# Post-norm rounds regrouped, two first pieces behind the last transposes, and one sum moved behind a split, in a single-core decoder layer

## The chip, the cores and the metric

One core of a Trainium2 chip runs the whole layer. The metric is the device time of one execution in microseconds (us). The kernel before takes 1078.08 us, the median of 3 runs (1076.54 to 1078.99).

## What is computed

One layer of a decoder trunk, in float32, for 1024 positions of width 1024. Cut to what matters here:

```python
y = mixing_sublayer(h, ...)                  # pooling and dilated attention, then @ w_out
x = x + gt_m * rms_norm(y, g_post_mix)       # residual after the first sub-layer
h = rms_norm(x, g_pre_ffn) * (1.0 + sc_f) + sh_f
up = h @ w_up                                # 1024 x 1024 by 1024 x 5632
gate, val = up[..., :D_FF], up[..., D_FF:]   # D_FF = 2816
gate = causal_conv3(gate, conv_w) + conv_b
y = (gelu(gate) * val) @ w_down
x = x + gt_f * rms_norm(y, g_post_ffn)
```

`rms_norm` divides a row by the root of its mean square. Everything that the change touches lies between `@ w_out` and the first blocks of `h @ w_up`.

## The kernel before, in words

**Splits.** A float32 operand of a large product is split into a high and a low part, and three matmuls (high by high, high by low, low by high) replace one. ScalarE (ACT) writes the high part as a rounded copy (L120), VectorE (DVE) the low part as a difference (L167). A pair of such parts of a 128x512 weight is called a piece here. PE can use the high part as soon as ACT has written it, and needs the low part one matmul later.

**The out-projection and the first norm.** Positions are cut into 8 tiles of 128. `y_part` (L592 to L594) issues three matmuls of a tile's product with `w_out`; 8 of these make a tile, in two of the eight accumulator banks. Tiles 0 to 3 have the bank pairs 0-1, 2-3, 4-5 and 6-7. `stats(t)` is called after each tile and works a round: it loads the residual's rows `xr` (L881, issued by SyncE's queue, SP), squares y of tile t on ACT with a sum (L884), squares x1 of tile t-1 on ACT (L889), takes the root (L149), refines both reciprocals in five tiny DVE instructions (L163, L156 to L159), writes x1 = y times its factor times a gate row (L894, which is the last to read the tile's banks), adds the residual (L895), stores x1 (L896), and scales x1 of tile t-1 into `xr` (L898). That last result is what the up-projection needs.

**The turns.** The scaled rows must be transposed. A turn (`x_turn`, L905) is 8 PE transposes of two tiles' `xr` into banks 6 and 7, and `h_split` copies them out on ACT (L913, 4 copies) into `raw_a` or `raw_b`, which hold a quarter of the transposed h each. `TURN_AT` says before which slot each turn stands: slot (t, n) is the n-th `y_part` of tile t, and from t = 8 on the n-th group of three matmuls (L1016 to L1018) of the first products of the up-projection, block c = t - 8. The block with c = 3 writes into banks 6 and 7, so it starts after the last turn's copies. The first turn writes into the banks of y's tile 3, so it starts after that tile's L894.

**The first blocks of the up-projection.** `h @ w_up` is done with seven products in place of eight on half-size blocks, so sums of the blocks of h (`sums`, L940), and sums of weight quarters (`start_sum`, L950, for chunk 0; `total`, L1137, on GpSimd, POOL, later) are needed. A product (n, c) is product n of column chunk c: 12 matmuls (L1066 to L1068) that take a left factor (`s` for n = 5, `s2` for 6, `s4` for 3, `s3` for 7) and a weight piece. Products (5,0), (6,0), (3,0) and (7,0) come first, then (5,1) and (6,1). `evac` adds a finished product into accumulators in SBUF (L1075 to L1085). The block `b` (`parts("22")`, 128x2048) is split for a later product. A ring of piece buffers is filled in turn: the last five are `p1` and four pieces of `more`, and `more` lies in the storage of `raw_a`, so it can be written once b's split has read that.

**Order.** On PE, ACT, DVE and POOL the order is the order of the code (`manual_schedule`); each engine works its instructions strictly in turn. Two more constants place work between the slots: at `FIRST_T`, (10,2), stand the sums and pieces of products (5,0) and (6,0) (two L950, then p from `raws` and p from `t2r`), and at `LAST_X`, (8,6), the round that only scales x1 of tile 7, and a one-element Gelu (L1008) that makes ACT load its Gelu table.

Of the kernel before, what the change touches and what calls it, by code (L numbers as in the profile page):

```python
# [68 lines left out]


NCONST = _const_layout()
LAST_X = (8, 6)
FIRST_T = (10, 2)
TURN_AT = ((5, 4, 0, 0), (6, 2, 0, 1), (6, 7, 1, 0), (7, 2, 1, 1), (8, 3, 2, 0), (8, 7, 2, 1), (9, 7, 3, 0), (10, 3, 3, 1))
# [27 lines left out]
def block_kernel(ctx: ExitStack, tc: tile.TileContext, x, pos, cols, rows, consts, w_ada_a, w_ada_b, w_in_u,  # L102
                 w_in_p, w_pool, w_out, w_up, w_down, out):
    nc = tc.nc
    cp = ctx.enter_context(tc.tile_pool(name="cp", bufs=1))
# [7 lines left out]
    PS = pp.tile([P, 8, 512], F32, name="PS")  # L113
# [25 lines left out]
    one = cp.tile([P, 1], F32, name="one")  # L139
# [362 lines left out]
    gtg = cp.tile([P, D], F32, name="gtg", tag="gtg")  # L502
# [81 lines left out]
    def y_bank(t):  # L584
        return 2 * t if t < 4 else 2 * ((t - 4) % 3)
# [281 lines left out]
    if True:  # L867
        ep = mid.enter_context(tc.tile_pool(name="ep", bufs=1))
        st8 = [{} for _ in range(NT)]
# [2 lines left out]
            for n in range(lo, hi):  # L872
                y_part(t, n % 2, n // 2)

        def stats(t):
            q = ep.tile([P, 2], F32, name="q1", tag="q1", bufs=3)
            n, d = 0, st8[t] if t < NT else None
            if t < NT:
                yv = PS[:, y_bank(t):y_bank(t) + 2, :].rearrange("p a b -> p (a b)")
                d["xr"] = ep.tile([P, D], F32, name="xr", tag="xr", bufs=6)  # L880
                nc.sync.dma_start(d["xr"], xv[:, t])  # L881
                d["x1"] = ep.tile([P, D], F32, name="x1", tag="x1", bufs=2)
                junk = ep.tile([P, D], F32, name="junk", tag="junk")
                nc.scalar.activation(junk, yv, AF.Square, accum_out=q[:, 0:1])  # L884
                n = 1
            if t:
                e = st8[t - 1]
                junk = ep.tile([P, D], F32, name="junk", tag="junk")
                nc.scalar.activation(junk, e["x1"], AF.Square, accum_out=q[:, n:n + 1])  # L889
                e["rx"] = n  # L890
                n += 1
            r = rsqrt(q[:, 0:n], root(q[:, 0:n], n), n)
            if t < NT:
                nc.vector.scalar_tensor_tensor(d["x1"], yv, r[:, 0:1], gtg, op0=ALU.mult, op1=ALU.mult)  # L894
                nc.vector.tensor_add(d["x1"], d["x1"], d["xr"])  # L895
                nc.sync.dma_start(x1v[:, t], d["x1"])  # L896
            if t:
                nc.vector.tensor_scalar_mul(e["xr"], e["x1"], r[:, e["rx"]:e["rx"] + 1])  # L898

        def x_turn(m, r):  # L900
            for i in range(4):
# [40 lines left out]
        ring, at, W, TR = [], {"p": 0, "r": 0}, {}, {}  # L942
# [5 lines left out]
        def start_sum(n, o, a, b):  # L948
            TR[n, 0] = o
            nc.vector.tensor_tensor(o, a, b, ALU.add)  # L950
# [9 lines left out]

        TURNS = {(t, n): (m, r) for t, n, m, r in TURN_AT}
        up_load(0)
# [3 lines left out]
        if True:  # L966
# [5 lines left out]
            root(cat[0][0][:, S - 1:S].bitcast(F32), scale=0.0)  # L972
            for t in range(3):
                y_mm(t, 6, 8)
                stats(t)
            for t in range(3, NT):
                for n in range(8):
                    slot((t, n))
                    y_mm(t, n, n + 1)
                stats(t)  # L980
            for c in range(AHEAD + 1):
                if c + 2 <= AHEAD:
                    up_load(c + 2)
                if c == 2:
                    raws = [rp.tile([P, 2, 512], F32, name="raws", tag="raw") for _ in range(2)]
                    raws = [t[:, i] for t in raws for i in range(2)]
                    for i in range(4):
                        nc.sync.dma_start(raws[i], w_up[0, :, i])
                    b11, b21, b12, b22 = raws
                    t2r = cp.tile([P, 512], F32, name="t2r", tag="macc")  # L990
                    p0 = r2.tile([P, 4, 512], F32R, name="p0", tag="r2b")
                    ring += [(p0[:, i], p0[:, i + 1]) for i in (0, 2)]
                    TR["t4", 0] = b21
                for n in range(8):
                    slot((8 + c, n))
                    if (8 + c, n) == FIRST_T:
                        start_sum("t1", b11, b11, b12)
                        start_sum("t2", t2r, b11, b22)
                        start_piece("t1", b11)
                        start_piece("t2", t2r)  # L1000
                    if (8 + c, n) == TURN_AT[-2][:2]:
                        sums(lo_t, range(4))
                        parts("s1", lo_t)
                        parts("s2", lo_t)
                    if (8 + c, n) == LAST_X:
                        stats(NT)
                        gelu = cp.tile([P, 1], F32, name="gelu")
                        nc.scalar.activation(gelu, one, AF.Gelu_apprx_tanh)  # L1008
# [7 lines left out]
                    nc.tensor.matmul(o, wh, ah, start=n % 4 == 0, stop=False)  # L1016
                    nc.tensor.matmul(o, wh, al, start=False, stop=False)
                    nc.tensor.matmul(o, wl, ah, start=False, stop=n % 4 == 3)  # L1018
# [3 lines left out]
            p1 = fp.tile([P, 2, 512], F32R, name="p1")  # L1022
# [35 lines left out]
            def product(n, c):  # L1058
                a, w = USES[n]
                wh, wl = W.pop((w, c))  # L1060
                used[n, c] = idle.pop(0)
                o = bank(used[n, c])
                for k in range(4):
                    ks = slice(k * P, (k + 1) * P)
                    ah, al = side(a, k)
                    nc.tensor.matmul(o, wh[:, ks], ah, start=k == 0, stop=False)  # L1066
                    nc.tensor.matmul(o, wh[:, ks], al, start=False, stop=False)  # L1067
                    nc.tensor.matmul(o, wl[:, ks], ah, start=False, stop=k == 3)  # L1068
# [33 lines left out]
            more = r1.tile(half, F32R, name="more", tag="rb2")  # L1102
# [16 lines left out]
    if True:  # L1119
# [134 lines left out]
        for hf, c in ((0, GATE_AT), (1, GATE_AT + 3)):  # L1254
            i = steps.index((5, c))
# [46 lines left out]

        prep_up(5, 5)
        parts("22", all_t)
        more = r1.tile([P, 8, 512], F32R, name="more", tag="rb0")
        ring += [(more[:, 2 * i], more[:, 2 * i + 1]) for i in range(4)] + [(p1[:, 0], p1[:, 1])]
        prep_up(6, 6)
        evac(7, 0)
        for i, (n, c) in enumerate(steps):
# [20 lines left out]
            if (n, c) == (5, NC_FF - 1):  # L1330
                more = r2.tile([P, 8, 512], F32R, name="tail", tag="r2c")
# [145 lines left out]
```

## Time and profile before

| what | value |
| --- | --- |
| median of 3 runs | 1078.08 us |
| the profiled execution: its own time | 1077.65 us |
| the profiled execution: its span | 1075.9 us |
| PE busy, share of the span | 1036.6 us, 96% |
| DVE busy | 850.9 us, 79% |
| ACT busy | 479.4 us, 45% |
| POOL busy | 223.1 us, 21% |
| mean granted PE clock | 0.992 |

The span is what the trace covers, and 1.75 us of the execution's own time lie round it. Times within the trace are counted from the span's start. A row of the timeline has the start, the duration, the engine, the line, the operation with out<-in, the shape and the count, and in brackets the idle time of the engine before it with what released it. PE matmuls are pipelined: a 128x512 matmul is shown with 0.39 us, but the next starts 0.23 us later. A row with x2, x4 or x8 holds so many instructions in succession. Names of buffers are those of the program, and `PS` is the accumulator.

### The profile page before, as it was taken

To read this page: it belongs to the slowest core of one execution; us is meant where nothing else is said; L and a number is where in the kernel's file an instruction comes from. 1 tells how busy PE (TensorE), PEld (TensorE's weight loads), DVE (VectorE), ACT (ScalarE), POOL (GpSimd) and SP (SyncE) were. 2 spreads that over 40 slices of the span, in tenths; PEclk is the share of its full clock that TensorE was granted. 3 is DMA by queue.
4 is the path that set the end of the run, shared out by engine and by line. 5 is a ranking of instruction groups with operands and counts; after the bars stand their busy time and mean duration, and the time that the engine had idled before them with its cause. 6 is when DMAs were issued, how large, how long until landed. Compare 5 with 4: busy or idle time off the path is not lost.

```text
span 1075.9 us, 15437 instructions
## 1 busy us (share of the span) xinstructions
PE 1036.6 (96%) x5174; PEld 875.5 (81%) x5174; DVE 850.9 (79%) x1845; ACT 479.4 (45%) x964; POOL 223.1 (21%) x132
## 2 busy tenths in 40 slices
PE   4999999999999989899999999999999999999997
PEld 4988988899888778677888888888878878888886
DVE  7975467875558668899999888979789999756897
ACT  6764333433354459543433333433323365544542
POOL 0000000000000000063433333333235425103460
PEclk9999999999999999899999999999999999999999
DMA  9552446362221163323344424344534889566663
GB/s 356 215 176 59 121 112 192 90 189 77 60 85 48 50 235 119 116 88 128 121 163 140 164 93 160 119 143 167 170 117 138 282 283 377 170 190 218 202 205 118
DMA packets 85148, 168.34 MB, mean 156 GB/s; under 512 B 9158, under 2 KB 25926, under 8 KB 81356
## 3 DMA queue, kind: packets, MB, share of 16 engines
q1 hardware_dynamic: 85068, 167.35, 46.9%
q8 instruction: 41, 0.67, 0.3%
q14 instruction: 39, 0.32, 0.1%
HBM read 134.47 MB, written 32.84 MB: 156 GB/s over the span
## 4 chain that ended last, share of the span: by engine, by line
PE 73%; DVE 13%; DMA 5%; ACT 5%; issue 3%; SPq 0%; DVEq 0%; ACTq 0%
PE PS L1066 9%; PE PS L1068 9%; PE PS L1067 9%; PE PS L1360 6%; PE PS L1361 6%; PE PS L1359 6%; PE PS L218 5%; PE PS L220 4%; PE PS L219 4%; PE PS L707 3%; PE PS L677 2%; DMA mraw<-in_w_ada_b_dram 2%; DVE more L1133 2%; PE PS L697 1%; DVE acc L340 1%
## 5 line engine op out<-in xcount | busy, mean ns | idle before, releaser
L1137 POOL TENSOR_TENSOR raws<-rw 128x512 f32<-128x512 f32 x30 | 49.8, 1661 | 505.8 <-DVE p L167 443.1
L218 PE MATMUL PS<-wh,hh 128*128 128x384 f32 x336 | 124.6, 371 | 0.1
L220 PE MATMUL PS<-wh,hl 128*128 128x384 f32 x336 | 113.2, 337 | 0.0
L219 PE MATMUL PS<-wl,hh 128*128 128x384 f32 x336 | 112.9, 336 | 0.0
L120 ACT ACTIVATE more<-raws 128x512 fp32r<-128x512 f32 x81 | 49.6, 624 | 70.7 <-PE PS L1067 54.3
L686 ACT ACTIVATE pm<-pm,nm 128x128 f32<-128x128 f32 (+1 forms) x96 | 42.4, 443 | 68.1 <-DVE nm L684 44.7
L1133 DVE TENSOR_TENSOR more<-raws,more 128x512 fp32r<-128x512 f32 x75 | 68.3, 913 | 3.4 <-ACT more L120 3.4
L218 PEld LDWEIGHTS PS<-wh,hh 128*128 128x128 f32 x336 | 63.4, 189 | 8.3 <-issue 4.8
L219 PEld LDWEIGHTS PS<-wl,hh 128*128 128x128 f32 x336 | 63.5, 189 | 0.6 <-issue 0.5
L220 PEld LDWEIGHTS PS<-wh,hl 128*128 128x128 f32 x336 | 63.1, 188 | 0.0
L1086 ACT ACTIVATE cv<-GG,col 128x1024 f32<-128x1024 f32 x22 | 27.4, 1245 | 73.1 <-DVE GG L1085 73.1
L1068 PE MATMUL PS<-a,more 128*128 128x512 f32 x144 | 56.3, 391 | 0.9 <-DVE more L1133 0.9
L1066 PE MATMUL PS<-a,more 128*128 128x512 f32 x144 | 56.1, 390 | 0.0
L1067 PE MATMUL PS<-a,more 128*128 128x512 f32 x144 | 56.0, 389 | 0.0
L680 DVE CUSTOM_DVE_ANT_0 pm<-PS,cst 128x128 f32<-128x128 f32 (+1 forms) x96 | 30.8, 347 | 30.6 <-PE PS L677 23.8
L1172 ACT ACTIVATE cv<-cv 128x1024 f32<-128x1024 f32 x22 | 23.4, 1062 | 62.9 <-DVE cv L1170 62.9
L1360 PE MATMUL PS<-tail 128*128 128x512 f32 x128 | 50.0, 391 | 0.5 <-DVE tail L167 0.4
L1361 PE MATMUL PS<-tail 128*128 128x512 f32 x128 | 49.8, 389 | 0.0
L1359 PE MATMUL PS<-tail 128*128 128x512 f32 x128 | 49.8, 389 | 0.0
L1168 DVE SCALAR_TENSOR_TENSOR cv<-GG,col,cv 128x1023 f32<-128x1023 f32 x22 | 35.8, 1628 | 10.8 <-ACT cv L1086 10.7
L1137 POOL TENSOR_TENSOR t2r<-raws,rw 128x512 f32<-128x512 f32 x14 | 29.5, 2110 | 68.3 <-DVE p L1133 45.1
L511 DVE SCALAR_TENSOR_TENSOR macc<-mraw,cact,macc 128x512 f32<-128x512 f32 x42 | 31.3, 746 | 15.2 <-DMA mraw<-in_w_ada_b_dram 14.9
(390 smaller groups left out, 3104.2 us busy)
## 6 DMA issues: line engine op xcount, KB each, us to landing
rw<-in_w_up_dram SPq DMA_DIRECT2D x21, 1024.0 KB
gscr<-VV SPq DMA_DIRECT2D x66, 256.0 KB
mraw<-in_w_ada_b_dram SPq DMA_DIRECT2D x48, 256.0 KB
R<-in_w_down_dram SPq DMA_DIRECT2D x48, 256.0 KB
raw<-in_w_in_u_dram SPq DMA_DIRECT2D x24, 384.0 KB
wa<-in_w_ada_a_dram SPq DMA_DIRECT2D x8, 1024.0 KB
R<-gscr SPq DMA_DIRECT2D x27, 256.0 KB
raws<-in_w_up_dram SPq DMA_DIRECT2D x25, 256.0 KB
```

Of the source, the lines that this page charges most:

```text
L120: nc.scalar.activation(o, i, AF.Copy)
L218: nc.tensor.matmul(o, a, wh[:, c0:c0 + 384], start=k == 0, stop=False)
L219: nc.tensor.matmul(o, a, wl[:, c0:c0 + 384], start=False, stop=False)
L220: nc.tensor.matmul(o, b, wh[:, c0:c0 + 384], start=False, stop=k == 7)
L1066: nc.tensor.matmul(o, wh[:, ks], ah, start=k == 0, stop=False)
L1067: nc.tensor.matmul(o, wh[:, ks], al, start=False, stop=False)
L1068: nc.tensor.matmul(o, wl[:, ks], ah, start=False, stop=k == 3)
L1133: nc.vector.tensor_tensor(wl, r, wh.bitcast(F32), ALU.subtract)
L1137: nc.gpsimd.tensor_tensor(t, a, b, ALU.add)
L1359: nc.tensor.matmul(o, gh[:, ts_], wh, start=k == 0, stop=False)
L1360: nc.tensor.matmul(o, gh[:, ts_], wl, start=False, stop=False)
L1361: nc.tensor.matmul(o, gl[:, ts_], wh, start=False, stop=k == KD - 1)
```

## The change

Four things are edited.

1. `stats` takes two lists, the tiles whose y it normalises and the tiles whose x1 it scales. A table `ROUNDS` says what each call does: y of tile 0; y of 1 and 2; y of 3 with x1 of 0 and 1; y of 4 with x1 of 2 and 3; and from there on y of t with x1 of t-1. There are 8 rounds in place of 9. x1 has four buffers in place of two.
2. The first turn moves from slot (5,4) to slot (5,5).
3. `LAST_X` moves from (8,6) to (8,7), where a turn stands too, so that the last scaling follows that turn's copies; the one-element Gelu moves behind `parts("s3")`. `FIRST_T` moves from (10,2) to (10,5), so that the first sums and pieces follow the last turn at (10,3).
4. `evac(3, 0)` and the sum for `t4` (one L1078 and one L950) move behind `parts("22")`, the split of b; and the ring gets `p1` ahead of the four pieces of `more`.

The diff, cut to its core:

```diff
-LAST_X = (8, 6)
-FIRST_T = (10, 2)
-TURN_AT = ((5, 4, 0, 0), (6, 2, 0, 1), ...
+LAST_X = (8, 7)
+FIRST_T = (10, 5)
+ROUNDS = {0: ((0,), ()), 2: ((1, 2), ()), 3: ((3,), (0, 1)), 4: ((4,), (2, 3)), 5: ((5,), (4,)), 6: ((6,), (5,)),
+          7: ((7,), (6,))}
+TURN_AT = ((5, 5, 0, 0), (6, 2, 0, 1), ...
...
-        def stats(t):
-            q = ep.tile([P, 2], F32, name="q1", tag="q1", bufs=3)
+        def stats(ys, xs):
+            n = len(ys) + len(xs)
+            q = ep.tile([P, 4], F32, name="q1", tag="q1", bufs=3)
...
+            for i, t in enumerate(ys):
...
-                d["x1"] = ep.tile([P, D], F32, name="x1", tag="x1", bufs=2)
+                d["x1"] = ep.tile([P, D], F32, name="x1", tag="x1", bufs=4)
...
+            for i, t in enumerate(xs, len(ys)):
                 junk = ep.tile([P, D], F32, name="junk", tag="junk")
+                nc.scalar.activation(junk, st8[t]["x1"], AF.Square, accum_out=q[:, i:i + 1])
             r = rsqrt(q[:, 0:n], root(q[:, 0:n], n), n)
...
                     if (8 + c, n) == LAST_X:
-                        stats(NT)
-                        gelu = cp.tile([P, 1], F32, name="gelu")
-                        nc.scalar.activation(gelu, one, AF.Gelu_apprx_tanh)
+                        stats((), (NT - 1,))
...
             start_piece("t3", b12)
             pairs_of("s3")
             parts("s3", all_t)
+            gelu = cp.tile([P, 1], F32, name="gelu")
+            nc.scalar.activation(gelu, one, AF.Gelu_apprx_tanh)
             product(7, 0)
             evac(6, 0)
-            evac(3, 0)
-            start_sum("t4", b21, b21, t2r)
...
         prep_up(5, 5)
         parts("22", all_t)
+        evac(3, 0)
+        start_sum("t4", b21, b21, t2r)
         more = r1.tile([P, 8, 512], F32R, name="more", tag="rb0")
-        ring += [(more[:, 2 * i], more[:, 2 * i + 1]) for i in range(4)] + [(p1[:, 0], p1[:, 1])]
+        ring += [(p1[:, 0], p1[:, 1])] + [(more[:, 2 * i], more[:, 2 * i + 1]) for i in range(4)]
```

Lines in the changed kernel are two or so further down for the same code: the copy L120 is L122 there, the difference L167 is L169, the first norm's L884, L889, L894, L895 and L898 are L888, L891, L895, L896 and L899, the turn's copies L913 are L914, and the sums L940 and L950 are L941 and L951.

Three places show what moves. The first is DVE in the rounds of tiles 1 and 2. In the rows of before, x_4172, x_4196 and x_4223 are x1 of tiles 0, 1 and 2:

```order
L894 SCALAR_TENSOR_TENSOR x_4196<-PS,r_4205,gtg 128x1024
L895 TENSOR_TENSOR x_4196<-x_4196,xr 128x1024
L898 TENSOR_SCALAR xr<-x_4172,r_4205 128x1024
L163 TENSOR_SCALAR v<-q_4220 128x2
L156 RECIPROCAL r_4232<-sd 128x2
L157 TENSOR_TENSOR v<-v,r_4232 128x2
L158 SCALAR_TENSOR_TENSOR v<-v,r_4232 128x2
L159 SCALAR_TENSOR_TENSOR r_4232<-v,r_4232 128x2
L894 SCALAR_TENSOR_TENSOR x_4223<-PS,r_4232,gtg 128x1024
L895 TENSOR_TENSOR x_4223<-x_4223,xr 128x1024
L898 TENSOR_SCALAR xr<-x_4196,r_4232 128x1024
```

The same place on DVE now, where x_4172, x_4202, x_4207 and x_4252 are x1 of tiles 0, 1, 2 and 3:

```order
L896 TENSOR_TENSOR x_4202<-x_4202,xr 128x1024
L895 SCALAR_TENSOR_TENSOR x_4207<-PS,r_4214,gtg 128x1024
L896 TENSOR_TENSOR x_4207<-x_4207,xr 128x1024
L165 TENSOR_SCALAR v<-q_4249 128x3
L158 RECIPROCAL r_4263<-sd 128x3
L159 TENSOR_TENSOR v<-v,r_4263 128x3
L160 SCALAR_TENSOR_TENSOR v<-v,r_4263 128x3
L161 SCALAR_TENSOR_TENSOR r_4263<-v,r_4263 128x3
L895 SCALAR_TENSOR_TENSOR x_4252<-PS,r_4263,gtg 128x1024
L896 TENSOR_TENSOR x_4252<-x_4252,xr 128x1024
L899 TENSOR_SCALAR xr<-x_4172,r_4263 128x1024
L899 TENSOR_SCALAR xr<-x_4202,r_4263 128x1024
```

Tiles 1 and 2 share one group of the tiny instructions, no scaling stands between them, and x1 of tiles 0 and 1 are scaled behind tile 3's read of its banks.

The second place is ACT from the turn of slot (8,7) to the first pieces. The 128x256 x4 rows are the turns' copies, `wh` is a weight's high part, s and s2h are left factors, and the two p rows are the first pieces. Before:

```order
L149 ACTIVATE sd<-q_4558,epst 128x1
L1008 ACT_TABLE_LOAD
L1008 ACTIVATE gelu<-one 128x1
L913 ACTIVATE raw_a<-PS,bcol_101,acol_100 128x256 x4
L120 ACTIVATE wh<-raw 128x1024
L913 ACTIVATE raw_b<-PS,bcol_101,acol_100 128x256 x4
L120 ACTIVATE s_4573<-s1t 128x4x256
L120 ACTIVATE s2h<-raw_a 128x2x256 x2
L120 ACTIVATE p_4656<-raws 128x512
L120 ACTIVATE p_4656<-t2r 128x512
L913 ACTIVATE raw_a<-PS,bcol_101,acol_100 128x256 x4
```

And ACT there now:

```order
L914 ACTIVATE raw_a<-PS,bcol_101,acol_100 128x256 x4
L891 ACTIVATE junk,q_4563<-x_4494 128x1024
L151 ACTIVATE sd<-q_4563,epst 128x1
L122 ACTIVATE wh<-raw 128x1024
L914 ACTIVATE raw_b<-PS,bcol_101,acol_100 128x256 x4
L122 ACTIVATE s_4576<-s1t 128x4x256
L122 ACTIVATE s2h<-raw_a 128x2x256 x2
L914 ACTIVATE raw_a<-PS,bcol_101,acol_100 128x256 x4
L122 ACTIVATE p_4644<-raws 128x512
L122 ACTIVATE p_4644<-t2r 128x512
```

The last raw_a copies have passed the two p pieces, and the table load has left this stretch; it stands now between the copies s3h and the high part of b.

The third place is DVE round the split of b, with the pieces of products (5,1) and (6,1) and `evac`'s rows. Before:

```order
L1076 TENSOR_TENSOR VV_4730<-UU,PS 128x512
L1078 TENSOR_TENSOR VV_4730<-VV_4730,PS 128x512
L950 TENSOR_TENSOR raws<-raws,t2r 128x512
L1133 TENSOR_TENSOR more<-raws,more 128x512
L167 TENSOR_TENSOR b_4828<-raw_a,b_4827 128x2048
L1133 TENSOR_TENSOR more<-t2r,more 128x512
L1081 TENSOR_TENSOR UU<-UU,PS 128x512
```

And DVE there now:

```order
L1076 TENSOR_TENSOR VV_4718<-UU,PS 128x512
L1133 TENSOR_TENSOR more<-raws,more 128x512
L169 TENSOR_TENSOR b_4816<-raw_a,b_4815 128x2048
L1078 TENSOR_TENSOR VV_4718<-VV_4718,PS 128x512
L951 TENSOR_TENSOR raws<-raws,t2r 128x512
L1133 TENSOR_TENSOR p_4715<-t2r,p_4715 128x512
L1081 TENSOR_TENSOR UU<-UU,PS 128x512
```

The two moved rows stand behind the split of b, and the piece that follows, product (6,1)'s, goes into p1 and no longer into `more`. The order on POOL is the same in both kernels. On SP one load of `xr` (tile 5's) is issued behind two more stores of x1.

More of the change, by code (lines that the diff above doesn't have):

```diff
@@ L873, in y_mm @@
                 y_part(t, n % 2, n // 2)
-        def stats(t):
-            q = ep.tile([P, 2], F32, name="q1", tag="q1", bufs=3)
-            n, d = 0, st8[t] if t < NT else None
-            if t < NT:
-                yv = PS[:, y_bank(t):y_bank(t) + 2, :].rearrange("p a b -> p (a b)")
+        def stats(ys, xs):
+            n = len(ys) + len(xs)
+            q = ep.tile([P, 4], F32, name="q1", tag="q1", bufs=3)
+            yv = {}
+            for i, t in enumerate(ys):
+                d = st8[t]
+                yv[t] = PS[:, y_bank(t):y_bank(t) + 2, :].rearrange("p a b -> p (a b)")
                 d["xr"] = ep.tile([P, D], F32, name="xr", tag="xr", bufs=6)
                 nc.sync.dma_start(d["xr"], xv[:, t])
-                d["x1"] = ep.tile([P, D], F32, name="x1", tag="x1", bufs=2)
+                d["x1"] = ep.tile([P, D], F32, name="x1", tag="x1", bufs=4)
                 junk = ep.tile([P, D], F32, name="junk", tag="junk")
[L884 to L887, printed above, removed]
+                nc.scalar.activation(junk, yv[t], AF.Square, accum_out=q[:, i:i + 1])
+            for i, t in enumerate(xs, len(ys)):
                 junk = ep.tile([P, D], F32, name="junk", tag="junk")
-                nc.scalar.activation(junk, e["x1"], AF.Square, accum_out=q[:, n:n + 1])
-                e["rx"] = n
-                n += 1
+                nc.scalar.activation(junk, st8[t]["x1"], AF.Square, accum_out=q[:, i:i + 1])
             r = rsqrt(q[:, 0:n], root(q[:, 0:n], n), n)
-            if t < NT:
-                nc.vector.scalar_tensor_tensor(d["x1"], yv, r[:, 0:1], gtg, op0=ALU.mult, op1=ALU.mult)
+            for i, t in enumerate(ys):
+                d = st8[t]
+                nc.vector.scalar_tensor_tensor(d["x1"], yv[t], r[:, i:i + 1], gtg, op0=ALU.mult, op1=ALU.mult)
                 nc.vector.tensor_add(d["x1"], d["x1"], d["xr"])
                 nc.sync.dma_start(x1v[:, t], d["x1"])
-            if t:
-                nc.vector.tensor_scalar_mul(e["xr"], e["x1"], r[:, e["rx"]:e["rx"] + 1])
+            for i, t in enumerate(xs, len(ys)):
+                nc.vector.tensor_scalar_mul(st8[t]["xr"], st8[t]["x1"], r[:, i:i + 1])
         def x_turn(m, r):
@@ L974, in block_kernel @@
                 y_mm(t, 6, 8)
-                stats(t)
+                if t in ROUNDS:
+                    stats(*ROUNDS[t])
             for t in range(3, NT):
@@ L979, in block_kernel @@
                     y_mm(t, n, n + 1)
-                stats(t)
+                stats(*ROUNDS[t])
             for c in range(AHEAD + 1):
```

2 lines of the change are left out of this document (1 added, 1 removed).

## The prediction

> **What bounds the kernel now.** I read the page's busy times first, then what PE waits for. The page's row and four rows of PE's waits (us in total, times, longest):
>
> ```profile
> PE 1036.6 (96%) x5174; PEld 875.5 (81%) x5174; DVE 850.9 (79%) x1845; ACT 479.4 (45%) x964; POOL 223.1 (21%) x132
> PE PS L1016 <- ACT raw_a L913: 3.7, 1, 3.7
> PE PS L905 <- DVE x L894: 3.6, 1, 3.6
> PE PS L1066 <- ACT more L120: 1.5, 1, 1.5
> PE PS L1066 <- DVE VV L1078: 0.8, 1, 0.8
> ```
>
> PE is busy for 96% of the span and paces the program, so a change gains what PE stops waiting. Both large waits lie in the stretch that is edited. The timeline of PE shows where: the last `y_part` before the first turn, the turn, the last turn, both sides of the second gap, the first matmul of product (7,0), a short wait in (5,1), and the first matmul of (6,1).
>
> ```profile
> 396.00 0.39 PE L594 MATMUL PS<-wh,cat 128*128 128x512 f32 x1
> 400.04 1.97 PE L905 MATMUL PS<-cst,xr 128*128 128x128 f32 x8 [3.64 <-DVE x L894]
> 436.19 1.03 PE L905 MATMUL PS<-cst,xr 128*128 128x128 f32 x8
> 440.27 0.39 PE L1018 MATMUL PS<-a,wl 128*128 128x512 f32 x1
> 444.36 0.80 PE L1016 MATMUL PS<-a,wh 128*128 128x512 f32 x1 [3.70 <-ACT raw_a L913]
> 460.86 0.39 PE L1066 MATMUL PS<-s3h,more 128*128 128x512 f32 x1
> 464.45 0.50 PE L1068 MATMUL PS<-s,more 128*128 128x512 f32 x1 [0.26 <-DVE more L1133]
> 468.47 0.50 PE L1066 MATMUL PS<-s2h,more 128*128 128x512 f32 x1 [1.46 <-ACT more L120]
> ```
>
> The table by stretches (busy us of each engine, then granted PE clock, DMA share, GB/s) shows what each gap costs besides itself:
>
> ```profile
> 400.00:406.00 6.00, 5.96 (x18) 5.07 (x19) 4.98 (x9) 4.32 (x8) 0.00 (x0) 0.50 0.22 87
> 444.40:450.40 6.00, 6.00 (x14) 4.73 (x15) 5.12 (x5) 4.41 (x8) 0.85 (x1) 0.51 0.00 0
> 450.00:470.00 20.00, 18.03 (x76) 13.96 (x75) 18.09 (x21) 9.16 (x12) 6.03 (x3) 0.99 0.09 27
> 470.00:490.00 20.00, 19.21 (x84) 15.24 (x83) 19.22 (x21) 7.70 (x12) 12.98 (x8) 1.00 0.37 120
> ```
>
> After each large gap PE runs 6.0 us at half clock and loses half of that, 3.0 and 2.9 us. After the wait of 1.46 us the clock stays. So the first gap costs 3.64 + 3.0 = 6.6 us and the second 3.70 + 2.9 = 6.6 us, 13.2 together. The other thing to see is DVE: 18.09 of 20 us busy behind the second gap, 19.22 of the next 20. A PE that comes 13 us earlier meets an engine there with hardly any room.
>
> **The rounds and the first gap.** DVE's rows for rounds 0 to 3, and ACT's square of x1:
>
> ```profile
> 384.72 1.23 DVE L895 TENSOR_TENSOR x<-x,xr 128x1024 f32<-128x1024 f32 x1 [1.01 <-DMA xr<-in_x_dram]
> 387.22 0.17 DVE L163 TENSOR_SCALAR v<-q 128x2 f32<-128x2 f32 x1 [1.28 <-ACT junk L889]
> 388.41 1.28 DVE L894 SCALAR_TENSOR_TENSOR x<-PS,r,gtg 128x1024 f32<-128x1024 f32 x1
> 389.73 1.23 DVE L895 TENSOR_TENSOR x<-x,xr 128x1024 f32<-128x1024 f32 x1
> 390.88 0.75 DVE L898 TENSOR_SCALAR xr<-x,r 128x1024 f32<-128x1024 f32 x1
> 398.70 1.28 DVE L894 SCALAR_TENSOR_TENSOR x<-PS,r,gtg 128x1024 f32<-128x1024 f32 x1
> 386.04 1.06 ACT L889 ACTIVATE junk<-x 128x1024 f32<-128x1024 f32 x1 [3.45 <-DVE x L895]
> ```
>
> Each round waits for the square of the x1 that the round before made (1.28 idle in this one), so tile 3's banks are read only at 398.70 to 399.98, and the turn starts at 400.04. Now: round 0's add ends at 385.95 as before. Tiles 1 and 2 need no x1, so their tiny group (387.22 to 388.41, 1.2 us, less without a wait for the root) ends by 387.1. L894 to L895 is 1.32 us and L895 to the next 1.15, so two pairs take 4.9 and end at 392.0. The squares of x1 of tiles 0 and 1 and of tile 3's y, 1.2 us each, lie on ACT beside that. Another group, 1.2, L894 and L895 of tile 3, 2.5: 395.7. Two scalings, 0.7 each: 397.1 at the latest. PE ends its last `y_part` at 396.2, and one more (three matmuls at 0.23) stands ahead of the turn now: 396.9. I take no wait, with bounds of 0 and 1 us, since this chain has no slack and no excess. The half clock goes too: **6.6 us** off.
>
> Hidden: the x1 buffers cost only memory. SP's load of tile 5's `xr` goes behind two stores but is needed two rounds (10.3 us between 388.41 and 398.70) later.
>
> **The last turns.** ACT's rows from the table load to b's high part and the copy for product (6,1), then DVE's:
>
> ```profile
> 428.75 1.28 ACT L1008 ACT_TABLE_LOAD   x1
> 442.77 0.63 ACT L120 ACTIVATE p<-t2r 128x512 fp32r<-128x512 f32 x1
> 443.30 1.91 ACT L913 ACTIVATE raw_a<-PS,bcol,acol 128x256 f32<-128x256 f32 x4
> 457.65 1.99 ACT L120 ACTIVATE s3h<-raw_b 128x1024 fp32r<-128x1024 f32 x2
> 460.07 1.90 ACT L120 ACTIVATE b<-raw_a 128x2048 fp32r<-128x2048 f32 x1
> 467.79 0.63 ACT L120 ACTIVATE more<-t2r 128x512 fp32r<-128x512 f32 x1 [5.82 <-DVE b L167]
> ...
> 433.05 1.22 DVE L167 TENSOR_TENSOR wl<-raw,wh 128x1024 fp32r<-128x1024 f32 x1 [2.52 <-ACT wh L120]
> 443.43 0.69 DVE L167 TENSOR_TENSOR p<-t2r,p 128x512 fp32r<-128x512 f32 x1
> 445.25 1.23 DVE L940 TENSOR_TENSOR s1t<-raw_a,raw_b 128x1024 f32<-128x1024 f32 x1 [1.13 <-ACT raw_a L913]
> 458.72 2.36 DVE L167 TENSOR_TENSOR s3l<-raw_b,s3h 128x1024 fp32r<-128x1024 f32 x2 [0.25 <-ACT s3h L120]
> 462.50 0.69 DVE L1078 TENSOR_TENSOR VV<-VV,PS 128x512 f32<-128x512 f32 x1
> 463.11 0.69 DVE L950 TENSOR_TENSOR raws<-raws,t2r 128x512 f32<-128x512 f32 x1
> 463.71 0.69 DVE L1133 TENSOR_TENSOR more<-raws,more 128x512 fp32r<-128x512 f32 x1
> 464.31 3.38 DVE L167 TENSOR_TENSOR b<-raw_a,b 128x2048 fp32r<-128x2048 f32 x1
> ```
>
> The last copies start at 443.30 only because the p copies ahead of them on ACT wait for DVE's sums; the transposes had been issued at 436.19. In front of the p copies they run at 436.19 - 6.6 + 1.0 = 430.6 to 432.5, and PE comes to them at 440.27 + 0.23 - 6.6 = 433.9. The second gap is gone with its half clock: **6.6 us** more, and the cover is 1.4 us.
>
> **What is late next.** DVE's chain from `wl` to p runs without idle time. `wl` came behind the table load (1.28, and 0.20 for the one-element Gelu), so it moves by 6.6 + 1.5 = 8.1 to 425.0, and p ends at 444.12 - 8.1 = 436.0. `s1t` follows at once, 9.1 us earlier than 445.25. PE is 13.2 earlier: DVE is behind by 4.1. First victim, product (7,0): PE arrives at 460.86 - 13.2 = 447.7; the first half of s3h is done at 448.55 + 1.0, so it waits some 1.9; the first half of s3l at 449.6 + 1.2 = 450.8, another 0.9. PE is now 10.4 ahead of its old time.
>
> Second victim, product (6,1). Its waits before (1.46, and 0.26 in product (5,1)) are absorbed, so PE arrives at 468.47 - 1.7 - 10.4 = 456.4. Its piece goes to p1, which nobody holds (product (3,0), its last reader, ends right ahead of (7,0)), so the copy no longer waits for b. But it copies `t2r`, which POOL writes, and POOL may write it only when the moved L950 has read it. POOL's rows:
>
> ```profile
> 463.97 1.58 POOL L1137 TENSOR_TENSOR t2r<-raws,rw 128x512 f32<-128x512 f32 x1 [18.72 <-DVE raws L950]
> 465.50 3.35 POOL L1137 TENSOR_TENSOR raws<-rw 128x512 f32<-128x512 f32 x1
> ```
>
> So the wait goes on: b's split, L1078, L950, then POOL, then ACT. ACT: s3h at 448.55, plus 460.07 + 1.90 - 457.65 = 4.3, plus the load that now stands between, 1.4: b's high part is done at 454.3 (DVE is through with L1133 at 463.71 - 1.21 - 9.1 + 0.6 = 454.0, so the load costs 0.3 here). b's low part: 3.38 beside POOL in the trace; with POOL idle it is bounded by s3l, 2.36 for two halves of the same total size. POOL can't start before it ends now, so I take 2.3: 456.6. L1078 0.6, then 0.86 from the start of L950 to POOL (463.11 to 463.97), POOL 1.58, 0.10 to ACT, and 0.68 from its start to PE (467.79 to 468.47): 460.4. Against 468.47 that is **8.1 us earlier**; PE idles 4.0 us there. [...]
>
> An idle of 4.0 us is longer than the two that brought half clock, so I expect it again: at most 6.0 us as in the table, 2.9 lost; at least nothing. The restart is then full work, and I take one half of that, 3.0 us at half clock or 1.5 lost. The wait of 0.8 that PE had behind this point (on L1078) swallows as much. So 0.7 comes off (bounds 0 and 2.1). [...]
>
> Behind this, DVE and POOL do the same work, shifted, so the lead of PE stays to the end. **Sum:** 13.2 - 2.8 (product 7,0) + 1.7 - 4.0 (product 6,1) - 0.7 = 7.4 us. The profiled execution's 1077.65 (span 1075.9 and 1.75 round it) would be 1070.25; it lies 0.43 below the median, so on the median 1078.08 - 7.4 = 1070.7.
>
> **Rivals.** A: the gain is kept. If POOL's sum or the moved L950 isn't what ends last at (6,1), there is no wait and no half clock: 8.1 + 4.0 = 12.1, 1066.0. For it: b's old dependency is gone. Against it: the row at 463.97 names L950 as the releaser. Chance 0.14.
>
> B: the change doesn't do what it says at the first turn, since the longer chain of round 3 (three squares, two scalings behind L894) ends 3 us later than I summed, for example by a late load as in the 1.01 of 384.72. Then gap and half clock stay, the DVE chain keeps 6.6, and 7.4 - 6.6 = 0.8 is left: 1077.3. Against it: only if the chain slips by 3 us. Chance 0.10.
>
> C, on the other side: half clock lasts. From product (7,0) on PE waits again and again (1.9, 0.9, 4.0). If the throttle takes the whole DVE-paced stretch from 450 to 490 as idle, 40 us at half clock lose 20; the 4.0 at (6,1) and the 0.8 behind lie within that, so 15.2 come off the 8.1 without a clock term: 7.1 slower, 1085.2. It is slower by over 2.2 from (8.1 + 2.2 + 4.8) x 2 = 30 us at half clock on. For it: three waits within 13 us. Against it: both old gaps were over in 6 us, and the stretch behind keeps PE busy 19.21 of 20. Chance 0.06.
>
> **Numbers.** Forecast 0.70: 1070.7, its own range from 1069.2 (no half clock, and the old 0.8 gone) to 1074.6 (b at 3.38 as in the trace, 1.1 more; half clock of 6.0 us, 1.4 more; a first turn that waits 1 us, and 0.4 for the sum of my roundings). The range reaches down to A, 1065.8, and leaves out B and C, 0.16. A measurement of this kernel can tell some 0.2%, 2.2 us. Faster: forecast and A, 0.84. Same: B, 0.10. Slower: C, 0.06.
>
> **What would show it.** Right: no wait over 1 us at the first turn and none at block c = 3; PE clock 1.0 from 400 to 440; new waits of near 2 and 1 us at product (7,0) on s3h and s3l; one of 4 us at (6,1), released by the copy from `t2r`, with POOL's `t2r` behind L1078 and L951; b's split at 2.3. Wrong: a wait of 3 us or more at the first turn (B), none at (6,1) (A), half clock beyond 470 (C).

## The result and the profile after

The changed kernel took 1073.19 us (median of 6 runs, 1068.81 to 1074.54) against 1078.92 for the kernel before (6 runs): a ratio of 0.994, 95% interval 0.9917 to 0.9963, or 5.7 us less. Timed a second time as it is, it took 1071.46 (6 runs) against 1078.19 (20 runs): 0.9948, interval 0.9929 to 0.9967, 6.7 us less. The forecast was 7.4 us less, with a range from 1065.8 to 1074.6.

The profiled execution took 1068.81 us, with a span of 1067.0, so 8.9 us less than the span of before. Not all of that is the change's. Both traces have a common mark just ahead of it, ACT's first square of y of tile 0. In the kernel before:

```profile
380.09 1.03 ACT L884 ACTIVATE junk<-PS 128x1024 f32<-128x1024 f32 x1 [0.30 <-PE PS L594]
```

In the changed kernel:

```profile
378.49 1.03 ACT L888 ACTIVATE junk<-PS 128x1024 f32<-128x1024 f32 x1 [0.29 <-PE PS L596]
```

The code ahead of that row is the same, and it came 1.6 us earlier here by chance: in the eleven traces of this study the row lies anywhere between 377.73 and 382.65. From the row to the span's end the kernel before takes 1075.9 - 380.09 = 695.8 us and the changed one 1067.0 - 378.49 = 688.5, which is 7.3 less. In the trace of the second timing it is 689.0, 6.8 less. From here on places in traces are also given as us behind this first square, since that leaves the scatter of the start out.

What PE waits for now (us in total, times, longest), the three largest of the rows that are new:

```profile
PE PS L1066 <- ACT p L122: 2.0, 1, 2.0
PE PS L1066 <- ACT s3h L122: 1.6, 1, 1.6
PE PS L1067 <- DVE s3l L169: 0.8, 1, 0.8
```

The rows of 3.7 and 3.6 us that bounded this part before are gone. On PE's timeline the first turn follows the `y_part` matmuls without idle time. Product (5,0) begins with two short waits, products (7,0) and (6,1) wait longer, and between the latter two some matmuls are shown with 0.63 us in place of 0.39, where the granted clock is halved (0.51 from 451.0 to 454.5):

```profile
395.30 1.03 PE L906 MATMUL PS<-cst,xr 128*128 128x128 f32 x8
...
438.16 0.50 PE L1066 MATMUL PS<-s,p 128*128 128x512 f32 x1 [0.30 <-ACT UU L122]
438.98 0.50 PE L1067 MATMUL PS<-s,p 128*128 128x512 f32 x1 [0.32 <-DVE s L169]
...
448.79 0.49 PE L1066 MATMUL PS<-s3h,more 128*128 128x512 f32 x1 [1.58 <-ACT s3h L122]
450.05 0.50 PE L1067 MATMUL PS<-s3l,more 128*128 128x512 f32 x1 [0.77 <-DVE s3l L169]
451.48 0.63 PE L1066 MATMUL PS<-s3h,more 128*128 128x512 f32 x1
...
459.19 0.50 PE L1066 MATMUL PS<-s2h,p 128*128 128x512 f32 x1 [2.04 <-ACT p L122]
460.33 0.50 PE L1068 MATMUL PS<-s2h,p 128*128 128x512 f32 x1 [0.41 <-DVE p L1133]
```

The table by stretches shows the clock (each row has the stretch, its length, the busy time of PE, PE's weight loads, DVE, ACT and POOL, then the granted clock, the DMA share and GB/s):

```profile
394.70:434.00 39.30, 39.23 (x205) 32.72 (x204) 34.75 (x57) 34.27 (x64) 0.01 (x1) 1.00 0.43 157
447.20:451.00 3.80, 1.46 (x6) 1.01 (x6) 2.92 (x3) 3.77 (x5) 0.00 (x0) 1.00 0.00 0
451.00:454.50 3.50, 3.50 (x11) 2.69 (x10) 2.96 (x5) 2.52 (x3) 0.00 (x0) 0.51 0.46 147
454.50:459.20 4.70, 2.67 (x13) 1.88 (x11) 2.57 (x4) 0.69 (x2) 1.99 (x2) 1.00 0.00 2
459.20:465.00 5.80, 5.39 (x15) 3.98 (x16) 5.80 (x6) 2.72 (x6) 5.72 (x5) 0.71 0.23 57
465.00:485.00 20.00, 20.00 (x90) 16.55 (x89) 18.96 (x22) 8.23 (x12) 11.77 (x7) 1.00 0.41 143
```

PE is busy for 39.23 of the 39.3 us of the first row, at full clock; in the kernel before it stood still twice over the same work. Half clock comes twice behind it, for about 3.4 us each. DVE's rows carry the rest:

```profile
391.37 1.28 DVE L895 SCALAR_TENSOR_TENSOR x<-PS,r,gtg 128x1024 f32<-128x1024 f32 x1
393.83 1.41 DVE L899 TENSOR_SCALAR xr<-x,r 128x1024 f32<-128x1024 f32 x2
...
423.23 1.22 DVE L169 TENSOR_TENSOR wl<-raw,wh 128x1024 fp32r<-128x1024 f32 x1
434.22 2.31 DVE L941 TENSOR_TENSOR s1t<-raw_a,raw_b 128x1024 f32<-128x1024 f32 x1
453.55 2.29 DVE L169 TENSOR_TENSOR b<-raw_a,b 128x2048 fp32r<-128x2048 f32 x1 [0.50 <-ACT b L122]
455.76 0.68 DVE L1078 TENSOR_TENSOR VV<-VV,PS 128x512 f32<-128x512 f32 x1
456.36 0.69 DVE L951 TENSOR_TENSOR raws<-raws,t2r 128x512 f32<-128x512 f32 x1
459.17 1.11 DVE L1133 TENSOR_TENSOR p<-t2r,p 128x512 fp32r<-128x512 f32 x1 [2.13 <-ACT p L122]
```

And ACT's and POOL's that go with them:

```profile
428.76 1.94 ACT L914 ACTIVATE raw_a<-PS,bcol,acol 128x256 f32<-128x256 f32 x4
449.70 1.28 ACT L1109 ACT_TABLE_LOAD   x1
458.51 0.63 ACT L122 ACTIVATE p<-t2r 128x512 fp32r<-128x512 f32 x1 [4.99 <-POOL t2r L1137]
...
433.99 1.46 POOL L1137 TENSOR_TENSOR raws<-rw 128x512 f32<-128x512 f32 x1 [433.55 <-DMA rw<-in_w_up_dram]
457.21 1.26 POOL L1137 TENSOR_TENSOR t2r<-raws,rw 128x512 f32<-128x512 f32 x1 [21.77 <-DVE raws L951]
```

The chain that the prediction named stands there in a row: b's split, L1078, L951, POOL's t2r, ACT's copy, PE.

### The profile page after: what moved, and what is told of

Same layout as the page of the kernel before. It is cut to its first block, busy times and chain, and to the rows that moved or that the text cites. A ratio compares the mean times of both kernels' runs of the same rounds, so it can differ in the third digit from the quotient of the medians.

```text
span 1067.0 us, 15433 instructions
## 1 busy us (share of the span) xinstructions
PE 1034.3 (97%) x5174; PEld 875.2 (82%) x5174; DVE 849.4 (80%) x1840; ACT 479.4 (45%) x963; POOL 223.3 (21%) x132
## 4 chain that ended last, share of the span: by engine, by line
PE 67%; DVE 17%; DMA 6%; issue 4%; ACT 4%; SPq 0%; DVEq 0%; POOL 0%; ACTq 0%; POOLq 0%
PE PS L1068 7%; PE PS L1067 7%; PE PS L1066 7%; PE PS L1362 6%; PE PS L1361 6%; PE PS L1363 6%; PE PS L220 5%; PE PS L222 4%; PE PS L221 4%; DMA gm<-in_w_ada_b_dram 3%; PE PS L709 3%; PE PS L679 2%; DVE more L1133 2%; PE PS L699 1%; DMA mraw<-in_w_ada_b_dram 1%
## 5 line engine op out<-in xcount | busy, mean ns | idle before, releaser
L122 ACT ACTIVATE more<-raws 128x512 fp32r<-128x512 f32 x79 | 48.2, 624 | 74.0 <-PE PS L1067 57.1
L1068 PE MATMUL PS<-a,more 128*128 128x512 f32 x136 | 53.2, 391 | 1.0 <-DVE more L1133 1.0
L1066 PE MATMUL PS<-a,more 128*128 128x512 f32 x136 | 52.9, 389 | 0.0
L1067 PE MATMUL PS<-a,more 128*128 128x512 f32 x136 | 52.9, 389 | 0.0
```

Source lines behind the costliest of these rows:

```text
L122: nc.scalar.activation(o, i, AF.Copy)
```

## The experiments

Theory: the two gaps overlap with one chain on DVE that starts before the last turn and sets the pace of PE from product (7,0) on, so what PE gains there is handed back wherever DVE is still behind; part 4 of the change puts two more DVE instructions and POOL into that chain. Rivals: each part brings its own share; or part 4 is what keeps the wait at (6,1) small. The table has the median of each with that of the kernel before in the same series, the ratio and its interval, and from the profiled execution the start of the third matmul of product (6,1) (the one that needs the low part of its piece), the start of the matmul that has 1500 others between the first square and itself, called the 1500th, and the span's end, all in us behind the first square.

| run | median, before, us | ratio (95%) | (6,1) | 1500th | end |
| --- | --- | --- | --- | --- | --- |
| before | 1078.08 (3 runs) | | 89.36 | 350.88 | 695.8 |
| the change | 1073.19, 1078.92 | 0.994 (0.9917 to 0.9963) | 81.85 | 343.57 | 688.5 |
| as_is | 1071.46, 1078.19 | 0.9948 (0.9929 to 0.9967) | 81.85 | 343.66 | 689.0 |
| rounds_only | 1070.66, 1078.19 | 0.9942 (0.9923 to 0.9961) | 82.69 | 344.94 | 692.6 |
| late_only | 1076.71, 1078.19 | 0.9986 (0.997 to 1.0001) | 86.28 | 347.75 | 693.7 |
| part4_off | 1070.90, 1078.19 | 0.9942 (0.9923 to 0.9961) | 81.02 | 342.49 | 688.7 |
| t4_back | 1072.34, 1078.89 | 0.9937 (0.9914 to 0.9959) | 81.02 | 342.50 | 687.7 |
| warm | 1070.93, 1078.89 | 0.993 (0.9908 to 0.9953) | 81.89 | 343.38 | 690.8 |
| gelu_late | 1069.07, 1078.89 | 0.9923 (0.9897 to 0.995) | 81.25 | 343.16 | 689.3 |
| b_low_act | 1068.54, 1077.65 | 0.9924 (0.9894 to 0.9953) | 79.12 | 340.57 | 689.0 |
| t4_back_gelu_late | 1070.74, 1077.65 | 0.9945 (0.9926 to 0.9965) | 81.03 | 343.06 | 688.3 |

In `warm`, whose 23 added matmuls are not counted, the numbers are those of the same matmuls as in the others. Added lines shift the numbers of those behind them: a product's first line, L1066 in the changed kernel, is L1068 in `rounds_only` and L1069 in `warm`.

**as_is.** No edit.

> The changed kernel as it is, timed again, to tell how large the gain is. Theory (the prediction's sum): 7.4 us less than the kernel before, with new waits of near 2 and 1 us at product (7,0) and 2 to 4 us at product (6,1). Rival: the first timing's 5.7 us is the true size, and the sum gave away 1 to 2 us too little.

Measured: 6.7 us less by the medians and 7.2 at the 1500th matmul. The profile repeats that of the first to 0.1 us at every place in the table but the end. So against the one trace of before the change is worth 7.2 or 7.3 us where it acts. By the medians the forecast's 7.4 lies within both intervals, and so does the rival's 5.7: they don't decide between the two.

**rounds_only.** The changed kernel with parts 3 and 4 undone:

```diff
-LAST_X = (8, 7)
-FIRST_T = (10, 5)
+LAST_X = (8, 6)
+FIRST_T = (10, 2)
...
                         stats((), (NT - 1,))
+                        gelu = cp.tile([P, 1], F32, name="gelu")
+                        nc.scalar.activation(gelu, one, AF.Gelu_apprx_tanh)
...
             parts("s3", all_t)
-            gelu = cp.tile([P, 1], F32, name="gelu")
-            nc.scalar.activation(gelu, one, AF.Gelu_apprx_tanh)
             product(7, 0)
             evac(6, 0)
+            evac(3, 0)
+            start_sum("t4", b21, b21, t2r)
...
-        evac(3, 0)
-        start_sum("t4", b21, b21, t2r)
...
-        ring += [(p1[:, 0], p1[:, 1])] + [(more[:, 2 * i], more[:, 2 * i + 1]) for i in range(4)]
+        ring += [(more[:, 2 * i], more[:, 2 * i + 1]) for i in range(4)] + [(p1[:, 0], p1[:, 1])]
```

> Only the rounds and the first turn's slot are changed; the last scaling, the first sums and pieces, the Gelu and the split of b stand as before. Theory (the stretches share one chain on DVE, so the parts overlap): the first gap goes with its half clock, the second gap stays at 3.7 us, and 6.6 to 7.6 us are gained, about all that the whole change gains. Rival (each part brings its own share of the net gain): clearly less than the whole change, about half, 3.5 us.

Measured: the second gap stands with its 3.70 us, though the half clock behind it lasted 3.4 us here and 6.8 in the trace of before, and (6,1) waits 1.4 us:

```profile
438.51 0.50 PE L1018 MATMUL PS<-a,wh 128*128 128x512 f32 x1 [3.70 <-ACT raw_a L914]
...
462.62 0.50 PE L1068 MATMUL PS<-s2h,more 128*128 128x512 f32 x1 [1.41 <-ACT more L122]
```

All the same (6,1) is 6.7 us earlier and the 1500th matmul 5.9, against 7.3 for the whole change. The rounds alone bring four fifths of it: the theory's side, though a little under its 6.6 to 7.6. PE's lead was 7.8 us in product (5,0), 1.1 of it from the shorter half clock, and fell again at the waits of products (5,1) and (6,1). In this execution 2.6 us more were lost around 400 us behind the first square, where PE waited 0.9 and 1.2 us and fell to half clock (matmuls shown with 0.63 us from 785.4 to 787.5), so the end is 3.2 us early only. This execution, 1075.31, was the slowest of the nine; their median, 7.5 us less, doesn't show that loss, and what decides it is open.

**late_only.** The changed kernel with the old rounds, the turn at (5,4), and part 4 undone as above:

```diff
-TURN_AT = ((5, 5, 0, 0), ...
+TURN_AT = ((5, 4, 0, 0), ...
-ROUNDS = {0: ((0,), ()), 2: ((1, 2), ()), 3: ((3,), (0, 1)), 4: ((4,), (2, 3)), 5: ((5,), (4,)), ...
+ROUNDS = {0: ((0,), ()), 1: ((1,), (0,)), 2: ((2,), (1,)), 3: ((3,), (2,)), 4: ((4,), (3,)), 5: ((5,), (4,)), ...
```

> Only the last scaling, the first sums and pieces and the Gelu are moved; rounds, first turn and the split of b as before. Theory: the first gap stays at 3.6 us with half clock, the second goes, product (7,0) waits 1.7 and 1.0 us in its place, and 4 to 5.5 us are gained. With the run of the rounds alone that makes more than the whole change gains. Rival (the second gap was worth its full 6.6 us): 6.6 us gained and no wait at (7,0).

Measured:

```profile
400.90 1.67 PE L906 MATMUL PS<-cst,xr 128*128 128x128 f32 x8 [3.43 <-DVE x L895]
...
456.75 0.50 PE L1066 MATMUL PS<-s3h,more 128*128 128x512 f32 x1 [1.58 <-ACT s3h L122]
458.01 0.50 PE L1067 MATMUL PS<-s3l,more 128*128 128x512 f32 x1 [0.76 <-DVE s3l L169]
466.47 0.51 PE L1066 MATMUL PS<-s2h,more 128*128 128x512 f32 x1 [1.33 <-ACT more L122]
```

The second gap is gone, the waits at (7,0) are there as with the whole change, and (6,1) and the 1500th matmul come 3.1 us earlier. That is under the theory's 4 to 5.5 and far under the rival's 6.6. The first 1.4 of it isn't the part's: the half clock behind the first gap lasted 3.4 us in this execution and 6.8 in that of before. So of a gap that cost 6.6 us of PE's time, 1.7 us were gained.

**part4_off.** The changed kernel with the last edits of `rounds_only` (those of `evac`, the sum and the ring) and nothing else.

> The changed kernel with its fourth part undone: the two moved DVE instructions ahead of the split of b again, and the ring as before. Theory (the moved sum holds POOL's t2r, and with it product (6,1), behind b): the wait of 2 to 4 us at (6,1) falls to about 1.5 us, and the gain over the kernel before is 9 to 10.3 us, 2 to 3 more than the change's. Rival (p1 ahead in the ring is what saves the copy for (6,1) from waiting on b): (6,1) waits as long or longer, and the gain is 5 us or less.

Measured: the wait at (6,1) is 1.44, but one of 1.19 comes in product (5,1) for a low part that the two instructions now hold up, and b's split takes 3.37 beside POOL, whose addition of 1.57 us starts at 454.92:

```profile
455.41 0.50 PE L1068 MATMUL PS<-s,more 128*128 128x512 f32 x1 [1.19 <-DVE more L1135]
459.42 0.50 PE L1066 MATMUL PS<-s2h,more 128*128 128x512 f32 x1 [1.44 <-ACT more L122]
477.36 0.47 PE L1066 MATMUL PS<-s2h,more 128*128 128x512 f32 x1 [0.80 <-DVE VV L1078]
...
455.27 3.37 DVE L169 TENSOR_TENSOR b<-raw_a,b 128x2048 fp32r<-128x2048 f32 x1
```

There was no half clock in the stretch: no matmul from 449 to 482 is shown with 0.63 us. The 1500th matmul is 1.1 us earlier than with the change, which is the theory's sign and not its size. 0.6 of that was lost again by the 1800th and the rest by the 2200th, so that the ends agree (688.7 against 688.5 and 689.0). The rival falls, since (6,1) waits less without p1 ahead in the ring. Over the whole time part 4 neither gains nor costs what can be told.

**t4_back.** Part 4 with the ring as changed, only the two instructions put back:

```diff
             evac(6, 0)
+            evac(3, 0)
+            start_sum("t4", b21, b21, t2r)
...
         parts("22", all_t)
-        evac(3, 0)
-        start_sum("t4", b21, b21, t2r)
```

> The changed kernel with only the two moved DVE instructions put back ahead of the split of b; p1 stays first in the ring. Theory (the moved sum is what holds POOL's t2r): POOL writes t2r some 3 us earlier, beside b's split, which then takes 3.3 us; the first matmul of (6,1) no longer waits 2 us, its third waits a little for the low part behind b, and 1.5 to 2.8 us are gained at (6,1) over the change. Whether they last is open: with part 4 undone as a whole 2.4 us gained there were 1.1 us some 40 us later and none at the end. Rival (the split of b itself is the wait): (6,1) starts no earlier than in the changed kernel.

Measured on PE, DVE and POOL:

```profile
462.42 0.50 PE L1068 MATMUL PS<-s2h,p 128*128 128x512 f32 x1 [1.85 <-DVE p L1135]
479.38 0.47 PE L1066 MATMUL PS<-s2h,more 128*128 128x512 f32 x1 [0.80 <-DVE VV L1078]
...
457.28 3.38 DVE L169 TENSOR_TENSOR b<-raw_a,b 128x2048 fp32r<-128x2048 f32 x1
...
456.93 1.58 POOL L1139 TENSOR_TENSOR t2r<-raws,rw 128x512 f32<-128x512 f32 x1 [18.56 <-DVE raws L951]
```

POOL's t2r does come earlier (75.5 us behind the first square, 78.7 with the change), and (6,1)'s first matmul no longer waits. Its third waits 1.85 for the low part behind b's longer split, so the product is 0.8 us earlier, not 1.5 to 2.8, and 0.8 of wait on L1078 comes back. At the 1500th matmul 1.1 us remain, and at the end 0.8 to 1.3. Both theory and rival had half: the moved sum held the high part, and b's split on DVE would have held the low part almost as long.

**warm.** PE's idle time is filled, so that no half clock comes:

```diff
                 used[n, c] = idle.pop(0)
                 o = bank(used[n, c])
+                for _ in range({(7, 0): 9, (6, 1): 14}.get((n, c), 0)):
+                    fill = side("s4", 0)[0]
+                    nc.tensor.matmul(o, fill[:, 0:P], fill, start=True, stop=True)
```

> The changed kernel with PE's idle time filled: 9 matmuls ahead of product (7,0) and 14 ahead of (6,1), written to the bank that the product then starts afresh, so no result changes. Theory (the half clock behind the two waits costs what it loses, less what the next wait hides): the clock stays at 1.0; that behind (7,0) was hidden in the wait of (6,1), that behind (6,1) costs up to 1.7 us, so 0.7 to 1.7 us are gained just behind (6,1), and less at the end. Rival (DVE paces the whole stretch): the clock stays and nothing is gained, since the waits grow by as much.

Measured by stretches (the clock is 1.00 in each) and on PE:

```profile
451.00:459.00 8.00, 7.43 (x33) 5.68 (x32) 6.44 (x8) 6.34 (x7) 0.00 (x0) 1.00 0.19 66
459.00:470.00 11.00, 10.18 (x44) 7.83 (x43) 8.85 (x10) 4.19 (x8) 8.53 (x6) 1.00 0.16 39
...
463.39 0.50 PE L1069 MATMUL PS<-s2h,p 128*128 128x512 f32 x1 [0.41 <-ACT p L122]
481.51 0.47 PE L1069 MATMUL PS<-s2h,more 128*128 128x512 f32 x1 [0.83 <-DVE VV L1081]
```

(6,1) starts when it did (80.74 behind the first square against 80.70), so the half clock behind (7,0) was wholly hidden. That behind (6,1) cost 1.6 us by the 420th matmul, some 16 us on, and only 0.2 at the 1500th matmul, because a wait of 0.83 on DVE's evacuation L1078 (L1081 in this kernel) takes its place, which the changed kernel no longer has. So the theory's 0.7 to 1.7 just behind (6,1) and less later is what came, and the reason that little is left is the rival's: there a wait on DVE grew by nearly as much. At the end this execution is 2.2 us behind the change (690.8 against 688.5), lost behind the 1740th matmul, far from the added ones; one trace doesn't tell why.

**gelu_late.** The one-element Gelu behind b's split:

```diff
-            nc.scalar.activation(gelu, one, AF.Gelu_apprx_tanh)
+            unit = one
...
         parts("22", all_t)
+        nc.scalar.activation(gelu, unit, AF.Gelu_apprx_tanh)
```

> The changed kernel with the one-element Gelu, and ACT's table load with it, behind the split of b instead of ahead of it. Theory (DVE's split of b waits 0.5 us for ACT's high part, which stands behind the load): b's split starts 0.5 us earlier, and (6,1) with it; 0.5 us gained there, and at most that at the end. Rival (the load costs nothing where the change puts it): the same times at (6,1).

Measured:

```profile
457.84 0.50 PE L1066 MATMUL PS<-s2h,p 128*128 128x512 f32 x1 [1.58 <-ACT p L122]
...
452.21 2.28 DVE L169 TENSOR_TENSOR b<-raw_a,b 128x2048 fp32r<-128x2048 f32 x1
```

b's split starts 74.5 us behind the first square, 0.6 earlier than with the change (75.1), and without its wait of 0.5 on ACT. (6,1) is 0.6 earlier and the 1500th matmul 0.4: the theory. The end, 689.3, is no earlier, as the theory allowed, and the median of 1069.07 can't be told from the change's, since the intervals overlap.

**b_low_act.** DVE's part of b's split, the subtraction, is left out; ACT copies b itself into the low part's place, so this kernel doesn't compute the layer:

```diff
-        parts("22", all_t)
+        for k, h, l in A["22"]:
+            copy(nc.scalar, h, SRC["22"][:, k:k + h.shape[1]])
+            copy(nc.scalar, l, SRC["22"][:, k:k + h.shape[1]])
```

> The changed kernel with the low part of b left out on DVE: ACT copies b itself into the low part's place, so that operand is a wrong value and DVE has 2.3 us less to do in the stretch. Theory (behind the last turn DVE paces PE, up to the wait on L1078 some 98 us behind the first square): DVE's chain to (6,1) is 2.5 to 2.8 us earlier, the wait of 2 us at (6,1) goes, no wait on L1078 comes in its place, and 2 to 2.8 us are gained over the change in the stretch, lasting. Rival (PE or POOL paces behind (6,1)): the wait on L1078 comes back with 0.8 us as in the runs with the sum put back, and no more than their 1.1 us are gained.

Measured:

```profile
474.40 0.47 PE L1066 MATMUL PS<-s2h,more 128*128 128x512 f32 x1 [0.79 <-DVE VV L1078]
```

(6,1) no longer waits, and the 1500th matmul is 3.0 us earlier, more than the theory's 2 to 2.8. The wait on L1078 is there after all, but 96.1 us behind the first square in place of 98.0 in `t4_back`: it moved with DVE's chain. That it moved is the theory's point, that it stayed is the rival's; the size, 3.0 against the rival's 1.1 at most, decides for DVE. By the end the lead is gone (689.0): 1.0 us around 400 us, and 2.5 us behind the 2880th matmul, where four short waits of 0.24 us stand in the output's last products. Whether these are this kernel's or this execution's one trace doesn't tell.

**t4_back_gelu_late.** Both mendings, `t4_back` and `gelu_late`, in one kernel.

> Both mendings together: the two moved DVE instructions ahead of b's split again, p1 first in the ring, and the Gelu behind b's split. Theory (both lie in one chain on DVE, which then runs into the wait on L1078): as with the sum put back alone, 1.1 us less than the change behind that wait, and at most 0.4 more from the load. Rival (their gains add up): 1.5 us or more less. In the whole time about 1069.5 to 1071.

Measured: (6,1) at 81.03, the 1500th matmul at 343.06, 0.5 earlier than with the change and 0.6 later than `t4_back` alone, the end at 688.3. The gains don't add up, which is the theory's side, though its 1.1 us wasn't reached either. What it has less than `t4_back` is half clock behind (6,1): that came here after a wait of 1.90 us, and not there after one of 1.85. By medians no version with the new rounds can be told from the change, or from another; `t4_back` has the earliest end behind the first square, 687.7, 0.8 to 1.3 us before the change's two traces.

## Why the prediction was right

Point by point, places behind the first square where times are compared.

**First gap, 6.6 us.** Right: PE is 6.7 us earlier from the turn on in each of the eight kernels with the new rounds. Tile 3's L895 starts at 391.37 and `xr` of tiles 0 and 1 are done at 395.24; the turn starts at 395.30 without idle time on PE, with 0.06 us to spare. The bounds of 0 and 1 us were needed, since this cover is nothing.

**Second gap, 6.6 us.** Right: the last copies run at 428.76, ahead of the p pieces, and PE crosses to block c = 3 without a wait. At the end of that block it is 13.4 us earlier, where 13.2 was predicted.

**The first victim.** Missed: it is product (5,0), not (7,0). Round its two waits, shown with 0.30 and 0.32 us, 1.2 us of the lead go, and it is 12.2 when PE comes to (7,0). In the kernel before, the low part of s was ready at 447.65 + 1.22 = 448.87 and PE used it at 452.92:

```profile
447.65 1.22 DVE L167 TENSOR_TENSOR s<-s1t,s 128x1024 fp32r<-128x1024 f32 x1
452.92 0.39 PE L1067 MATMUL PS<-s,p 128*128 128x512 f32 x1
443.53 1.72 POOL L1137 TENSOR_TENSOR raws<-rw 128x512 f32<-128x512 f32 x1 [443.09 <-DVE p L167]
```

That is 4.05 us of slack, and by the prediction's own sum PE came 4.1 nearer to DVE: the list of victims had to begin there. The longer `s1t` (below) then makes it a wait.

**DVE behind, waits at (7,0).** Predicted some 1.9 and 0.9 us, measured 1.58 and 0.77.

**The chain to (6,1).** Predicted 8.1 us earlier, measured 88.38 to 80.70, 7.7. Its terms: b's split 2.3, measured 2.29, with POOL idle until 457.21; L951 to POOL 0.86, measured 0.85; POOL 1.58, measured 1.26. Missed was `s1t`: at 434.22 it runs beside POOL's first sum (433.99) and takes 2.31 in place of 1.23. In the kernel before that sum ran at 443.53, while DVE waited for the copies. In `rounds_only`, where the second gap stands, (5,0) has neither of its two waits; in `as_is`, `late_only` and `part4_off`, where that gap is gone, it has both, 0.3 us each. The prediction moved DVE's chain and didn't ask what it would meet.

**The wait at (6,1), 4.0 us.** The start was right to 0.4 us and the wait wrong: 2.04. The step that failed is that the waits at (7,0) leave the clock alone. They brought 3.4 us of half clock, 1.7 us of PE's time. With that and the 1.2 at (5,0) PE came to (6,1) 2.4 us later than predicted (78.7 against 76.3 behind the first square). `warm` shows that the half clock cost nothing: what PE loses ahead of (6,1) only shortens its wait there.

**The clock behind (6,1), 0.7 us.** Half clock came, for 3.4 us where 3.0 was taken, and the wait of 0.8 behind it swallowed more than the 0.8 that the sum gave: between the 420th and the 440th matmul the lead grows by 1.3, so 0.2 net by `warm`.

**The sum, 7.4 us.** 7.3 and 7.2 at the 1500th matmul in two traces. The path is right, and that it comes so near is in part luck: the missed terms (`s1t` up, POOL and the clock down) nearly cancel, and the trace of before is a single one. Half clock behind its first gap lasted 6.8 us; in `late_only`, which has the same gap, it lasted 3.4 and PE was 1.4 us earlier behind it. Had it lasted 3.4 in the trace of before too, the gain by traces would be some 5.9 us, an estimate from these two traces. The medians, 5.7 and 6.7 less, leave that open. Rivals A, B and C didn't come: (6,1) did wait, the first turn did not, and half clock ended within 3.4 us each time. That parts 1 and 2 alone bring 5.9 of it, and that part 4 brings nothing that can be told, the prediction didn't say.

## What to carry to other kernels

When two waits of the engine that paces a program lie one behind the other, look for the chain on another engine that will be late once both are gone: here 13.4 us of waits and half clock were removed and 7.3 gained, and one part alone had 5.9. To time a change of half a per cent in one profile, count from a common row just ahead of it; the start of this program scatters by 5 us between executions. What lies behind that row scatters too, here by 1.4 us with the length of one stretch of half clock, so keep more than one trace of the kernel before. A moved chain meets other work: ask of each instruction that is moved what runs beside it at its new place.

## What the runs showed of the hardware

Half clock came after short waits too. In the changed kernel waits of 1.58 and 0.77 us, with one matmul between them, brought it for 3.4 us (clock 0.51 from 451.0 to 454.5); in `part4_off` waits of 1.58 and 0.76 at the same place didn't (no matmul from 449 to 460 is shown with 0.63 us, and those that didn't wait have 0.39 or 0.40). A wait of 1.85 in `t4_back` didn't (clock 1.00 from 462.4 to 470), and one of 1.90 at the same place in `t4_back_gelu_late` did (0.70, the mean from 462.4 to 468). In the kernel before, gaps of 3.64 and 3.70 us brought 6.8 us each (clock 0.50 from 399.1 to 405.9 and from 443.5 to 450.3); in `late_only` one of 3.43 at the first place and in `rounds_only` one of 3.70 at the second brought 3.4. What decides whether half clock comes, and for how long, these rows don't tell.

A DVE subtraction with two inputs in SBUF took 2.29 us when POOL was idle (b in the changed kernel, 453.55) and 3.38, 1.09 more, when POOL's addition of 1.58 us had begun 0.35 us before it (`t4_back`, 457.28 behind 456.93). Why it takes longer there, no run takes apart.
